# Two 1024-token super-tiles per streamed weight, with recurrence, sample states and attention interleaved between dense matmul pieces

## The chip, the cores and the metric

One Trainium2 chip, all eight NeuronCores, one launch. Core *c* takes prompt sequence *c* (2048 tokens) and sample sequences 16*c* to 16*c*+15 (8 new tokens each). The metric is the device time of the slowest core in microseconds (us). The kernels here sometimes ran in a second, slower state, in which the cores of one die (once of both) had a lower granted clock and took some per cent longer (one execution of the last version: clock 0.79 to 0.80 and 2623 to 2636 us on cores 0 to 3, 0.93 and 2397 to 2402 us on cores 4 to 7); only fast runs are compared here. A ratio is the mean time of one kernel's fast runs over the mean of the other's fast runs of the same rounds, on the same chip, so it is not quite the ratio of the medians that are quoted.

Engines: PE (TensorE, matmuls), PEld (its weight load), DVE (VectorE), ACT (ScalarE), POOL (GpSimd, which here mostly issues DMAs, the weights' casting ones above all) and SP (which issues other DMAs). The program gives each engine one list of instructions, in the order of issue, with waits for the others by semaphores; what that order can cost shows below, where PE's dense work stands 6.47 us behind four transposes that wait.

## The reference, cut to what matters

```python
D_MODEL, SEQ, DEPTH = 1024, 2048, 2
DEC_BATCH, DEC_SEQ = 128, 8                      # sample group: 1024 tokens over the chip
RET_HEADS, RET_DK, RET_DV, RET_CHUNK = 4, 256, 512, 128
SWA_HEADS, SWA_KV_HEADS, SWA_HEAD_DIM, WINDOW, D_FF = 16, 2, 64, 128, 2816

def step(s, qkv):                                # retention, one 128-token chunk
    qc, kc, vc = qkv
    scores = einsum('bihd,bjhd->bhij', qc, kc) * intra[None]
    o = einsum('bhij,bjhe->bihe', scores, vc)
    o = o + einsum('bihd,bhde->bihe', qc, s) * q_decay[None, :, :, None]
    s = s * chunk_decay[None, :, None, None] + einsum('bjhd,bjhe->bhde', kc * k_decay[None, :, :, None], vc)
    return s, o
# ... o is group-normed per head, gated by silu(h @ w_g), and projected by w_o
# layer 1: softmax attention over a window of 128 with one sink per head

for layer in range(DEPTH):
    hp, hs = rms_norm(xp, norm_mix[layer]), rms_norm(xs, norm_mix[layer])
    # layer 0: retention for the prompt (state starts at 0) and for the sample (state_ret given, returned updated)
    # layer 1: sliding-window attention for the prompt, and for the sample with its key/value cache
    xp, xs = xp + yp, xs + ys
    xp = xp + swiglu(rms_norm(xp, norm_ffn[layer]), ffn_w1[layer], ffn_w3[layer], ffn_w2[layer])
    xs = xs + swiglu(rms_norm(xs, norm_ffn[layer]), ffn_w1[layer], ffn_w3[layer], ffn_w2[layer])
```

The sample group's recurrent states are 16 x 4 matrices of 256 x 512 fp32 per core: 33.5 MB to read and as much to write.

## The kernel before

A small scheduler records each operation with the buffers that it reads and writes and derives the semaphore waits. The kernel walks over four 512-token tiles; for each it streams every weight from HBM (fp32, cast to bf16 by the DMA) through a ring of slots. The order in which the program issues is the order of each engine's list.

```python
for t in range(NPT):                     # NPT = 4 tiles of 512 tokens
    ...
    if last:                             # the sample group rides with tile 3
        R_ = layer0(cx, t, False, t % 2, rider=(scx, ...))   # projections share the weights
        layer0(scx, NPT, True, (t + 1) % 2, pre=R_)          # its states, alone
    else:
        layer0(cx, t, False, t % 2)
    for c_ in cxs: rmsnorm(c_, 1)        # a norm is issued in one block
    ffn(cxs, 0)
    rmsnorm(cx, 2)
    layer1(cx, t, False)
    if last: layer1(scx, NPT, True)      # sample attention, alone
    for c_ in cxs: rmsnorm(c_, 3)
    ffn(cxs, 1)

# layer0, the recurrence of head hd beside the projections of head hd + 1
for c in range(nch):
    c_main(hd, c)            # scores, mask, state update, output, group norm and gate
    if q_: q_.pop(0)()       # one projection piece of the next head
    if c > 0: c_tail(hd, c - 1)          # transposes of the chunk before

# the sample's states, one 256x512 state at a time, four buffers in and four out
issue_s0(u); issue_s0(u + 1); issue_s0(u + 2); issue_s0(u + 3)
act(S0bf[u2][:, a, :], S0[ui][:, a, :], AF.Copy, [S0b[ui]], [S0bfb[u2]])
mm(ob[:, :], Qz[:, a, b, :], S0bf[u2][:, a, :], ...)
stt(Sn[ui][:, a, :], S0[ui][:, a, :], cd, pk[:, :], ALU.mult, ALU.add, ...)
dma("pool", srs[b, hd]..., Sn[ui][:, :, :], [Snb[ui]], [], f"sn{ui}")

# attention, one 128-token block and head pair
act(rec[:, ri, :128], db_[:, :128], AF.Identity, ..., bias=esink[:, hp:hp + 1])
recip(rec[:, ri, 128:256], rec[:, ri, :128], ...)            # 128 columns, 128 times
tt(oT[:, hp, qs], nb_[:, :128], rec[:, ri, 128:256], ALU.mult, ...)
```

The softmax here doesn't subtract the row's maximum and nothing guards it: scores larger than these inputs give would overflow.

## Time and profile before

| | before |
|---|---|
| time, median of 3 runs | 2907.16 us (2906.66 to 2914.06) |
| PE busy | 2195 us of 2913 (75%) |
| DVE, ACT busy | 39%, 31% |
| granted clock, mean by core | 0.860 to 0.867 |
| FFN of a tile | 133 and 142 us |
| sample states, alone; sample attention, alone | 270 us; 115 us |

Two more lines of the page count what the weights cost, since the change halves their traffic: packets, bytes into the cores and mean rate, then the traffic of HBM.

```profile
DMA packets 293096, 336.42 MB, mean 115 GB/s; under 512 B 7184, under 2 KB 257808, under 8 KB 292752
...
HBM read 528.55 MB, written 46.79 MB: 198 GB/s over the span
```

A line of the stage tables (here and in the prediction) reads: stretch in us from the span's start, its length, then busy us and instruction count of PE, PEld, DVE, ACT and POOL, the mean granted clock (1.00, called full, is the highest in the records: 512-column matmuls start 0.216 us apart at it and 0.427 at 0.50, called half), the busy share of the DMA engines and GB/s. A timeline line reads: start, length, engine, program line, operation, output and inputs, count, and in brackets the idle time before it with what ended it. A line of waits reads: engine, tile and line that waited, `<-` what ended the wait; us in total, times, longest. In the lines and below: *rope* is the position-dependent rotation of queries and keys on VectorE (its products are `rt`), `sT` the masked scores of a chunk, `S_0`, `S_1` or `S` the buffers of the sample states and `S0f` a state's bf16 copy; the *carried state* is what the second super-tile's recurrence takes over from the first; a *bank* is one of the eight numbered pieces (0 to 7) of `ps`, the kernel's buffer in PSUM, into which PE's matmuls write.

### The profile page before, as it was taken

The page shows a single profiled execution, that of the slowest core. Times are in us where ns is not written, and L with a number is a line of the kernel's source. Part 1 is how long each engine was busy: PE and PEld are TensorE (multiplying, and loading weights), DVE is VectorE, ACT ScalarE, POOL GpSimd, SP SyncE. Part 2 cuts the span into 40 slices and gives each one's busy share as a digit, 9 for nine tenths or more (in the row PEclk, how much of TensorE's full clock was granted, in tenths as well). Part 3 has the DMA queues.
Part 4 walks back from the last instruction along what each step waited for, and adds up shares of the span by engine and source line. Part 5 has one row for each costly group of instructions (what it writes and reads, how often), then busy time and mean ns, then how long its engine had stood idle before and what let it go on. Part 6 is the DMA issues. An engine that isn't in the chain of part 4 may idle for free.

```text
span 2913.1 us, 36426 instructions; the slowest of 8 cores (2885.2 to 2913.1 us)
## 1 busy us (share of the span) xinstructions
PE 2194.7 (75%) x11759; PEld 1031.3 (35%) x11759; DVE 1130.9 (39%) x2050; ACT 895.0 (31%) x1678; POOL 257.3 (9%) x311
## 2 busy tenths in 40 slices
PE   4768876987789868887798689776654499762697
PEld 1323333433334343333243434333211245341353
DVE  4542127136431172265311631645345331271422
ACT  2441134114521251144211520445233221343211
POOL 0000100110001100100011001000111201000010
PEclk9889988998879999999798999898755689895698
DMA  9547881797549827974488369544787878625274
GB/s 197 81 60 101 122 125 30 102 141 149 86 60 138 130 36 108 145 152 73 73 116 129 46 102 139 100 73 77 205 292 264 235 112 127 98 32 111 43 113 97
DMA packets 293096, 336.42 MB, mean 115 GB/s; under 512 B 7184, under 2 KB 257808, under 8 KB 292752
## 3 DMA queue, kind: packets, MB, share of 16 engines
q0 software_dynamic: 256944, 272.89, 59.4%
q1 hardware_dynamic: 35968, 61.20, 6.8%
q8 instruction: 101, 1.65, 0.2%
q14 instruction: 83, 0.68, 0.1%
HBM read 528.55 MB, written 46.79 MB: 198 GB/s over the span
## 4 chain that ended last, share of the span: by engine, by line
PE 60%; DVE 14%; DMA 11%; issue 8%; ACT 6%; DVEq 1%; SPq 0%; ACTq 0%; POOL 0%; POOLq 0%
PE pb L415 59%; DMA wr<-w 5%; DVE arena L424 4%; DVE arena L433 4%; DMA arena<-st_in 4%; ACT arena L421 3%; DVE rstd L433 2%; ACT sq L421 1%; ACT L421 1%; PE pb L418 1%; DVE hT L427 1%; DMA xT<-xTp 1%; DVE arena L427 1%; DVE stat L594 1%; DMA wr<-wo 1%
## 5 line engine op out<-in xcount | busy, mean ns | idle before, releaser
L415 PE MATMUL pb<-hT,wr 128*128 128x512 bf16 x3776 | 911.9, 399 | 81.5 <-DVE hT L427 68.3
L415 PEld LDWEIGHTS pb<-hT,wr 128*128 128x128 bf16 x3776 | 379.4, 101 | 592.2 <-issue 202.9
L415 PE MATMUL pb<-arena,wr 128*128 128x512 bf16 (+1 forms) x2720 | 535.7, 362 | 47.3 <-DMA wr<-w 21.8
L421 ACT ACTIVATE arena<-pb 128x512 bf16<-128x512 f32 (+3 forms) x584 | 319.9, 559 | 718.1 <-PE pb L415 629.4
L415 PEld LDWEIGHTS pb<-arena,wr 128*128 128x128 bf16 x2720 | 255.6, 103 | 323.6 <-issue 84.9
L415 PE MATMUL pb<-arena 128*128 128x128 bf16 (+2 forms) x576 | 146.4, 358 | 277.8 <-DVE arena L424 151.7
L424 DVE TENSOR_TENSOR arena<-arena,pb 128x512 bf16<-128x512 f32 x220 | 133.7, 608 | 526.4 <-PE pb L415 505.3
L436 POOL DMA_DIRECT2D wr<-w x144 | 125.0, 869 | 1350.7 <-PE pb L415 1349.1
L421 ACT ACTIVATE sq<-xT 128x512 bf16<-128x512 f32 x160 | 93.2, 622 | 491.2 <-PE pb L415 335.2
L415 PE MATMUL pb<-wr,hT 128*128 128x512 bf16 x1024 | 234.1, 389 | 0.0
L424 DVE TENSOR_TENSOR xT<-pb,xT 128x512 f32<-128x512 f32 x96 | 66.4, 692 | 419.9 <-PE pb L415 419.9
L421 ACT ACTIVATE arena<-arena 128x512 bf16<-128x512 f32 (+1 forms) x192 | 109.4, 575 | 268.8 <-DMA arena<-st_in 135.0
L415 PEld LDWEIGHTS pb<-arena 128*128 128x128 bf16 x576 | 42.3, 104 | 357.7 <-issue 351.9
L415 PEld LDWEIGHTS pb<-wr,hT 128*128 128x128 bf16 x1024 | 102.4, 100 | 127.9 <-issue 14.7
L424 DVE TENSOR_TENSOR arena<-arena,cbt 128x512 bf16<-128x512 bf16 (+2 forms) x148 | 57.4, 389 | 207.5 <-ACT arena L421 206.6
L415 PE MATMUL pb<-sq,cbt 128*128 128x512 bf16 (+1 forms) x200 | 74.1, 397 | 83.6 <-ACT sq L421 76.9
L427 DVE SCALAR_TENSOR_TENSOR arena<-arena,pb 128x512 f32<-128x512 f32 x128 | 87.3, 687 | 114.4 <-PE pb L415 102.8
L433 DVE RECIPROCAL arena<-arena 128x128 f32<-128x128 f32 (+1 forms) x130 | 127.9, 984 | 2.3 <-ACT arena L421 1.9
L433 DVE RECIPROCAL rstd<-rtmp 128x512 f32<-128x512 f32 (+1 forms) x25 | 71.8, 2873 | 110.8 <-ACT rtmp L421 110.1
L424 DVE TENSOR_TENSOR arena<-arena 128x512 bf16<-128x512 f32 (+2 forms) x136 | 87.7, 666 | 63.1 <-ACT arena L421 63.1
L418 PE MATMUL pb<-cbt,arena 128*128 128x128 bf16 x464 | 45.5, 244 | 79.2 <-DVE arena L1086 46.5
L421 ACT ACTIVATE Sbf<-Sst 128x512 bf16<-128x512 f32 x128 | 75.2, 624 | 97.2 <-PE pb L415 58.6
(79 smaller groups left out, 1623.0 us busy)
## 6 DMA issues: line engine op xcount, KB each, us to landing
wr<-w POOLq DMA_DIRECT2D x112, 1024.0 KB, 12.2
arena<-st_in SPq DMA_DIRECT2D x64, 512.0 KB, 8.0
srs<-arena POOLq DMA_DIRECT2D x64, 512.0 KB, 7.9
wr<-wo POOLq DMA_DIRECT2D x30, 1024.0 KB, 9.6
wr<-wqk POOLq DMA_DIRECT2D x16, 1024.0 KB, 13.3
wr<-wv POOLq DMA_DIRECT2D x16, 1024.0 KB, 11.7
wr<-wg POOLq DMA_DIRECT2D x16, 1024.0 KB, 9.9
wr<-w POOLq DMA_DIRECT2D x16, 768.0 KB, 13.6
```

Source lines behind the costliest of these rows:

```text
L415: S.op("pe", lambda e: e.matmul(out, lhsT, rhs, start=start, stop=stop), r, w)
L418: S.op("pe", lambda e: e.transpose(out, in_, ident), r, w)
L421: S.op("act", lambda e: e.activation(out=out, in_=in_, func=func, bias=bias, scale=scale), r, w)
L424: S.op(eng, lambda e: e.tensor_tensor(out=out, in0=in0, in1=in1, op=op), r, w)
L427: S.op("dve", lambda e: e.scalar_tensor_tensor(out=out, in0=in0, scalar=scalar, in1=in1, op0=op0, op1=op1), r, w)
L433: S.op("dve", lambda e: e.reciprocal(out=out, in_=in_), r, w)
L436: S.op(eng, lambda e: e.dma_start(out=out, in_=in_), r, w, dsem=sem)
L594: S.op("dve", lambda e: e.bn_stats(out=st[:, 0:6], in_=ob), [obb], [sbf])
```

## The change

Its intent: stream each weight twice, not four times; put the sample group's states, its attention and the recurrence beside dense matmuls instead of alone; take the norms apart into steps between other pieces. The core of a diff that replaces nearly the whole program (cuts marked by `...`):

```diff
-        for t in range(NPT):
-            ... one tile of 512 tokens, as above
+        for s in range(2):                           # super-tiles of 2 x 512 tokens
+            ta, tb = T[2 * s], T[2 * s + 1]
+            self.ret_layer(s, cxs, scx if s == 0 else None, ...)
+            if s == 0:   # the sample states: pairs 0 to 15 beside this FFN
+                self.ffn(cxs, 0, [...], sideB)       # sideB -> ret_sample(range(0, 16), ...)
+            else:
+                self.ffn(cxs + [scx], 0, [...], None)
+            self.att_layer(s, cxs, scx if s == 1 else None, [...])
+            ...          # second FFN: sideD -> ret_sample(range(16, 32), ...) where s == 0
+def weave(main, side, lead=0.0):                     # side pieces spread by their stated costs
+    for p in main:
+        out.append(p); cm += p[0]
+        while k < len(side) and cs / ts_ <= cm / tm - 1e-9 + lead:
+            out.append(side[k]); cs += side[k][0]; k += 1
+# retention: the recurrence Rp(h, ti) woven into the projections P(next)
+            for c in range(4):
+                pcs.append((3, lambda n=n: r_o(n)))        # output product, group norm, gate
+                pcs.append((2, lambda n=n: r_su(n)))       # state, accumulated in PSUM banks 4 and 5
+                pcs.append((0.5, lambda n=n: r_sc(n + 1))) # scores of the next chunk, bank 7, mask on DVE
+                pcs.append((1, lambda n=n: r_tl(n - 1)))   # transposes of the chunk before, bank 7
+        # projections: query halves, then key halves, each pair of banks held until its second rope half
+            for which in range(2):
+                for half in range(2):
+                    pcs.append(qk_half(which, half))
+            for c in range(4):
+                pcs.append(vg("v", c))
+        ...
+        # second super-tile: carried state added on DVE
+                    self.tt(sb_[:, :, :], S2, si_[:, :, :], ALU.add, sbk + sib, sbb)
+# sample states: pairs of states, two buffers, updated and stored in place
+        st["S0"] = [self.M.tile(f"S0_{i}", [128, 2, 2, 512], F32, self.xoff[2] + i * 8192) for i in range(2)]
+            if a == 1:
+                for gg in range(2):
+                    self.dma("sp", out_v[...], t[:, gg, :, :], tb, [], f"s0_{i % 2}")
+                load(i + 2)
+# attention: 64-row matmuls, one reciprocal for four head pairs
+            self.tt(r0..., ps[:, 7, :]..., self.esink..., ALU.add, ...)
+            self.recip(r0[:, :], r0[:, :], r0b, r0b)       # 512 columns, 32 times
+# norms: three steps, each issued one piece later
+        self.nq += [s0, s1, s2]
```

## The prediction

Rival 1 went whole: a lower granted clock in the dense stretches, with its sign, with the reason for stretching the range upward (2290 plus 150 is 2440, the range ends at 2490) and with one reason for the chance of 0.97. In the paragraph before "The change part by part" the 3353 ns are those of DVE's reciprocal. Some terms lean on estimates. Tiled matmuls at 69 us instead of 138 suppose that pairs of them overlap, which the kernel before could not show, as it has none. The "about 0.04" for 32 columns is high (they start 0.026 to 0.027 us apart even at half clock). A semaphore hop, from the end on one engine to the start on the other, is a median 0.11 us from PE to DVE and 0.15 from DVE to PE in the trace before. The 35 us of half clock were not worked out from the trace, which shows clock 0.50 from 850 to 860 us, in and after a norm gap.

> **What bounds the kernel now.** I read in this order: cores and dies (is this run undisturbed?), the page's first lines and slices (which engine, when), the chain that ended last, a table of engine busy time by stage, the PE timeline inside single stages, and last the groups with their mean durations. The dies agree within 1 us, so nothing here is a slow state.
>
> The page, then the chain:
> ```profile
> span 2913.1 us, 36426 instructions; the slowest of 8 cores (2885.2 to 2913.1 us)
> ...
> PE 2194.7 (75%) x11759; PEld 1031.3 (35%) x11759; DVE 1130.9 (39%) x2050; ACT 895.0 (31%) x1678; POOL 257.3 (9%) x311
> ...
> PEclk9889988998879999999798999898755689895698
> ...
> PE 60%; DVE 14%; DMA 11%; issue 8%; ACT 6%; DVEq 1%; SPq 0%; ACTq 0%; POOL 0%; POOLq 0%
> ```
> PE is the bound engine, but 718 us of the span (2913 - 2195) it does nothing, and its clock dips wherever it idles; 40% of the chain is other engines and DMA. The stage table of core 2 (columns: stretch, its length, busy us and counts of PE, PEld, DVE, ACT, POOL, granted clock, DMA share, GB/s) shows where:
> ```profile
> 642.00:843.00 201.00, 154.87 (x721) 69.52 (x721) 103.41 (x205) 83.87 (x147) 13.10 (x15) 0.86 0.59 101
> 843.00:976.00 133.00, 123.10 (x536) 53.15 (x534) 29.15 (x39) 19.72 (x32) 15.63 (x18) 0.94 0.87 123
> 976.00:1090.00 114.00, 80.42 (x578) 44.85 (x575) 63.48 (x116) 51.97 (x107) 5.26 (x6) 0.88 0.40 63
> 1090.00:1232.00 142.00, 125.42 (x543) 53.50 (x542) 29.94 (x40) 25.35 (x40) 16.51 (x19) 0.94 0.87 124
> ...
> 2070.00:2340.00 270.00, 125.25 (x420) 42.97 (x420) 125.10 (x177) 91.67 (x153) 50.97 (x70) 0.60 0.86 265
> ...
> 2620.00:2735.00 115.00, 35.66 (x527) 26.91 (x524) 29.70 (x85) 36.23 (x96) 3.63 (x5) 0.57 0.48 93
> ```
> The first four lines are one 512-token tile: retention with its output projection, FFN, attention, FFN. The FFNs are dense; retention loses 46 us and attention 34. The last two lines are the sample group's recurrent states (bound by DMA at 265 GB/s) and its attention: 385 us in which PE works 161 us, at a clock near 0.6.
>
> The PE timeline gives the unit costs and shows what a gap is (start, length, line, operation, count, idle before and its releaser):
> ```profile
> 67.62 3.62 PE L415 MATMUL pb<-hT,wr 128*128 128x512 bf16 x16
> 71.08 0.71 PE L415 MATMUL pb<-arena 128*128 128x128 bf16 x4
> 78.14 0.58 PE L415 MATMUL pb<-arena 128*128 128x512 bf16 x1 [6.36 <-DVE arena L424]
> ...
> 2614.98 3.74 PE L415 MATMUL pb<-hTs_sb,wr 128*128 128x128 bf16 x64
> ```
> In the third line PE stands 6.36 us for the score mask, which DVE runs only after the rope of the next head. A warm 512-column matmul starts every 0.216 us ((3.62 - 0.38 for the last one's own length)/15), a 128-column one every 0.056 ((3.74 - 0.2)/63).
>
> [...]in 5 us windows the clock is 0.50 after each norm gap (850 to 860 us) and 1.00 from 865 on. [...]from 863 to 923 us all four cores of either die are busy 8 us or more of every 10, and all read 1.00. [...]the trace has 58 loads of 1283 ns. [...]the trace has 3353 ns for 128x512, against 692 for an add. [...]
>
> **The change part by part.**
> *PE work* (counts are of the built program of each kernel; they sum to 11759 and 10444). Before: 7780 with 512 columns, 3659 with 128, 320 with 32: 7780 x 0.216 + 3659 x 0.056 + 320 x about 0.04 = 1898 us warm. The measured 2195 us busy thus has about 297 us of half clock in it. After: 7388 full 512-column ones = 1596; 640 tiled 512-column ones (attention by 64 rows or columns, sample states by 32) are 138 us if they don't overlap and 69 in pairs, I take 105; 2224 with 128 = 125; 192 small = 8. Sum 1834. So the floor hardly moves (-64). The gain must come from the 718 us idle and the 297 us cold.
>
> *Weights.* Each is streamed twice, not four times (and wo, q1, wo1 again for the sample). Before, the DMA waits on wr are 5 to 6% of the chain; those 150 us go. The FFN of the first super-tile now also carries half the sample states: 34.6 MB of fp32 weights plus 33.5 MB of states, at the 300 GB/s or so that the queues reached (256944 packets in 59.4% of 16 engines is 108 ns for 2 KB read; 88 ns for 1.7 KB on the hardware queue) is about 220 us, in an FFN that takes PE 256 (1056 matmuls, and 16 pairs of states with 8 each). Tight; states are double-buffered and stored and loaded in place (two transfers of about 8 us each; a pair comes every 16 us and a buffer every second pair, so some 20 us are free). I allow 15 us in each of two FFNs.
>
> *Sample group.* 385 us alone become pieces between dense ones: their PE time is in the floor. Remains about 20 us where the sample attention's small steps outlast the few projections beside them.
>
> *Retention.* A 128-token chunk has 25 units (of 0.216 us) of projection beside 6.5 of recurrence: 6.8 us of PE. The norm-and-gate chain of a chunk in the trace (191.34 to 196.14) took 4.8 us with a table load, so it fits into a period. But the transposes of chunk n-1 stand right behind the scores of n+1 in the same PSUM bank, so each waits for the mask on DVE: 0.29 us plus two semaphore hops, plus what rope (12 x 0.69 per four chunks) has queued there. I put 1.3 us on each of 64 chunks: 83 us. ACT gets 92 table loads for 58 (Sqrt and Silu alternate 43 times for 24, counted in the program): +44 us, on an engine that has room (4.3 us of work plus 1.3 of load per 6.8).
>
> *Attention.* DVE per step: two masks 128x1024 bf16 about 0.7 each (0.417 at 512), add 0.69, reciprocal 3.35, multiply 0.69 = 6.1, with a hop 6.6 us; 8 steps 53 us. Beside it stand 27 us of PE (projections of the other tile) or 22 (wo1, which adds 6 us of DVE). DVE is the bound there: excess (53 - 27) + (59 - 22) = 63 per super-tile, 126 in all. The reciprocals themselves are no cheaper: 128 of 947 ns before (121 us), 32 of 3353 after (107).
>
> *Norms.* They no longer stop everything (10 us each before, 842.9 to 852.9), but their burst on DVE (3.35 + 8 x 0.67 = 8.7 us, behind a Sqrt table) holds up the adds that free two or four PSUM banks: I take 8 us where a two-bank projection follows (three a super-tile), 4 or less elsewhere: 40 per super-tile, 85 with the sample.
>
> *Ends.* Start 45 us (39 before; the constants that the first norm needs now queue behind four weight units), tail 20 (24 before). Between the super-tiles tile 3's input waits for tile 0's store: 15. Half clock after the remaining long gaps: 35.
>
> Sum: 1834 + 65 + 30 + 20 + 83 + 126 + 85 + 15 + 35 = 2293. Predicted **2290 us**.
>
> **The rivals.**
> 1. [...]
> 2. *In-order PE makes side pieces expensive.* Every wait in a side piece now stops dense work too; DVE (about 1090 us busy, as before) and ACT serve both. With 3 us per chunk instead of 1.3 and 10 us per norm: +150, 2440.
> 3. *Everything hides.* Tiled matmuls overlap by pairs, masks are ready, norms cost 2 us: 2130. Speaks for it: the before trace's DVE and ACT are idle 60%.
> 4. *DMA becomes the bound of the first super-tile's FFNs*: +40 us each.
>
> **Range and chances.** The terms for stalls sum to 394 us of which half is judgement: plus or minus 150 around 2290[...]: 2130 to 2490. [...]faster by over 2%: 0.97; within 2%: 0.02; slower: 0.01.
>
> **What would show it.** Right: PE busy near 1900 us with some 10,400 matmuls and 83% of the span; FFN stretches with PE at 95% and clock 1.00 while the states are loaded; attention stretches with DVE over 90% and PE near 50%; 92 table loads; PE waits in retention that name the mask (DVE into sT) in the transposes. Wrong: [...]waits of PE on state loads (rival 4); DVE under 80% in attention; PE waits on the gate chain larger than those on the mask.

## The result, and the profile after

The changed kernel took 2643.32 us (median of 4 runs, 2638.91 to 2651.96) where the kernel before took 2909.25 (4 runs, 2906.66 to 2914.06): ratio 0.9074, 95% interval 0.9039 to 0.9109. It is faster, as predicted, but by 266 us and not by 617; the time lies 353 us above the predicted 2290 and outside the range of 2130 to 2490.

The page of the changed kernel, the lines that answer to those shown of before, and two groups (line, engine, operation, names, shapes, count | busy us, mean ns | idle just before, and what ended it):

```profile
span 2650.9 us, 30100 instructions; the slowest of 8 cores (2614.8 to 2650.9 us)
...
PE 2096.1 (79%) x10444; PEld 927.8 (35%) x10444; DVE 1079.2 (41%) x1698; ACT 751.5 (28%) x1172; POOL 119.5 (5%) x227
...
PEclk9777777989878788898987988899999987889998
...
DMA packets 87220, 211.91 MB, mean 80 GB/s; under 512 B 10752, under 2 KB 13696, under 8 KB 83968
...
PE 57%; DVE 17%; DMA 13%; issue 7%; ACT 5%; DVEq 0%; SPq 0%; ACTq 0%; POOLq 0%
...
L506 ACT ACT_TABLE_LOAD x92 | 118.0, 1283 | 234.5 <-PE ps L499 99.9
...
L503 PE MATMUL ps<-cbt,u 128*128 128x128 bf16 x256 | 29.0, 246 | 138.8 <-DVE sT L509 130.8
```

The packets of all transfers are down from 293096 to 87220, their bytes from 336 to 212 MB, and PE idles 555 us instead of 718. But PE is busy for 2096 us, 262 more than the 1834 of the prediction's floor, with the very count of matmuls it named, so its clock must be lower than foreseen (this core's records read 0.50 for 489 us of the run and 0.81 for 477); DMA is a larger share of the chain than before (13% for 11%); and the transposes of the retention wait 131 us for the mask.

The stage table of core 3: retention, first FFN and attention of the first super-tile, then the same of the second.

```profile
0.00:491.00 491.00, 376.26 (x1664) 168.77 (x1665) 179.61 (x371) 194.50 (x309) 15.14 (x32) 0.82 0.29 57
491.00:839.00 348.00, 301.31 (x1217) 116.03 (x1215) 118.36 (x182) 78.07 (x106) 21.69 (x41) 0.85 0.66 157
839.00:1019.00 180.00, 120.85 (x549) 42.81 (x548) 123.47 (x114) 54.57 (x70) 5.81 (x11) 0.81 0.16 27
...
1377.00:1849.00 472.00, 332.73 (x1598) 151.74 (x1598) 211.36 (x381) 163.64 (x262) 13.03 (x25) 0.86 0.29 64
1849.00:2130.00 281.00, 267.94 (x1614) 137.02 (x1613) 83.13 (x140) 54.47 (x105) 23.14 (x42) 0.98 0.40 65
2130.00:2354.00 224.00, 140.39 (x972) 60.11 (x970) 155.91 (x176) 70.72 (x105) 6.77 (x13) 0.84 0.15 25
```

The second super-tile's FFN is what the prediction wanted everywhere: PE busy 268 of 281 us at clock 0.98, with the sample group's columns in it. The first super-tile's, with the sample states beside it, needs 67 us more. Two stages of retention make 963 us.

One period of the retention in detail (timeline of core 3; DVE between two matmul groups of PE):

```profile
1670.09 0.28 PE L499 MATMUL ps<-q_65,k_67 128*128 128x128 bf16 x2
...
1671.30 1.28 DVE L509 TENSOR_TENSOR rt<-ps,rope_52 128x512 f32<-128x512 f32 x2
...
1673.29 1.22 DVE L509 TENSOR_TENSOR Sbf_79<-ps,Sin_80 128x1024 bf16<-128x1024 f32 x1
1674.42 1.28 DVE L509 TENSOR_TENSOR rt<-ps,rope_52 128x512 f32<-128x512 f32 x2
...
1676.41 0.28 DVE L509 TENSOR_TENSOR sT<-ps,cbt 128x128 bf16<-128x128 f32 x1
...
1676.84 0.58 PE L503 MATMUL ps<-cbt,u 128*128 128x128 bf16 x4 [6.47 <-DVE sT L509]
```

The score product (first line) is done at 1670.4. Its mask (`sT`) needs 0.28 us of DVE, but stands there behind the gate of the last chunk, two rope halves and the addition of the carried state, all issued earlier. The transposes on PE don't need that mask at all: they write to the bank that the mask still has to read. For the kernel's scheduler bank 7 is one buffer, so it orders the transposes' writes behind the mask's read, and the 6.47 us are that order's price. Whether the order could be left out no run here shows: every kernel keeps it. All dense work stands behind the transposes.

The clock, in the stretches of that gap and after it:

```profile
1670.00:1675.00 5.00, 0.37 (x4) 0.10 (x1) 4.21 (x6) 0.58 (x1) 0.00 (x0) 1.00 0.39 77
1675.00:1682.00 7.00, 5.16 (x16) 2.17 (x17) 3.14 (x7) 0.60 (x1) 0.00 (x0) 0.52 0.00 0
```

PE is idle, keeps its full clock for some 5 us, and then has half the clock for 7 us, most of them with matmuls running. So a wait of 6.5 us is followed by 5.2 us of work at half speed, which is another 2.6 us lost.

The waits of core 3 (engine, line, releaser: us in total, times, longest), of PE, and of the queue that issues the state transfers:

```profile
PE ps L503 <- DVE sT L509: 130.8, 55, 6.8
...
PE ps L499 <- ACT S0f_109 L506: 63.7, 15, 12.2
```

```profile
SPq L123 <- DMA srs<-S_0_107: 114.4, 15, 13.6
SPq L123 <- DMA srs<-S_1_108: 95.1, 16, 9.8
```

The first line is the retention's transposes. In the others PE waits for the bf16 copy of a state (`S0f`), the copy for the state's load, and the load, issued into the buffer just stored, for the store to land: 6.8 us a time in the issuing queue, at most 13.6.

Last, the clock of the first run had a third value. On core 3 the records read 0.81 for 477 us of the run, on core 0 for 432, on cores 4 and 5 for 297, on cores 6 and 7 for 148. Core 0 and core 2 in the same stretch of the first retention:

```profile
150.00:250.00 100.00, 79.21 (x389) 38.25 (x395) 41.12 (x93) 48.28 (x75) 1.59 (x3) 0.88 0.19 37
...
150.00:250.00 100.00, 81.34 (x367) 37.55 (x367) 41.61 (x92) 44.59 (x69) 1.59 (x3) 0.75 0.20 38
```

Core 2 (the second line), at a mean clock of 0.75 for 0.88, needs more PE time for fewer matmuls: 81.3 us for 367 against 79.2 for 389. That is a lower granted clock, as in the prediction's rival 1, for a part of the run and some of the cores.

### The profile page after: what moved, and what is told of

It is laid out like the page before. It is cut to its first block, busy times and chain, and to the rows that moved or that the text cites. A ratio compares the mean times of both kernels' runs of the same rounds, so it can differ in the third digit from the quotient of the medians.

```text
span 2650.9 us, 30100 instructions; the slowest of 8 cores (2614.8 to 2650.9 us)
## 1 busy us (share of the span) xinstructions
PE 2096.1 (79%) x10444; PEld 927.8 (35%) x10444; DVE 1079.2 (41%) x1698; ACT 751.5 (28%) x1172; POOL 119.5 (5%) x227
## 2 busy tenths in 40 slices
DMA packets 87220, 211.91 MB, mean 80 GB/s; under 512 B 10752, under 2 KB 13696, under 8 KB 83968
## 4 chain that ended last, share of the span: by engine, by line
PE 57%; DVE 17%; DMA 13%; issue 7%; ACT 5%; DVEq 0%; SPq 0%; ACTq 0%; POOLq 0%
PE ps L499 56%; DMA S_0_107<-st_in 4%; DMA srs<-S_0_107 3%; DVE rt L509 2%; DMA S_1_108<-st_in 2%; DVE rstd L518 2%; PE ps L503 1%; DVE rec_124 L518 1%; DMA spt<-spar 1%; DVE h_44 L512 1%; DVE rec_125 L518 1%; ACT on L506 1%; DMA srs<-S_1_108 1%; DVE h_45 L512 1%; DVE stat L681 1%
## 5 line engine op out<-in xcount | busy, mean ns | idle before, releaser
L499 PE MATMUL ps<-h_44,wr 128*128 128x512 bf16 x1824 | 453.4, 408 | 35.2 <-DVE rt L509 10.4
L499 PE MATMUL ps<-h_45,wr 128*128 128x512 bf16 x1824 | 453.6, 407 | 26.0 <-DMA wr<-w 9.5
L499 PEld LDWEIGHTS ps<-h_44,wr 128*128 128x128 bf16 x1824 | 184.5, 103 | 282.9 <-issue 120.6
L499 PEld LDWEIGHTS ps<-h_45,wr 128*128 128x128 bf16 x1824 | 183.3, 103 | 273.7 <-issue 121.9
L499 PE MATMUL ps<-aT_105,wr 128*128 128x512 bf16 x704 | 170.9, 401 | 6.9 <-DVE x_62 L509 6.9
L509 DVE TENSOR_TENSOR aT_103<-s_104,ps 128x512 bf16<-128x512 f32 x88 | 60.4, 687 | 278.2 <-PE ps L499 242.9
L509 DVE TENSOR_TENSOR aT_105<-s_106,ps 128x512 bf16<-128x512 f32 x88 | 60.5, 687 | 262.6 <-PE ps L499 228.4
L499 PE MATMUL ps<-aT_103,wr 128*128 128x512 bf16 x704 | 164.5, 392 | 2.6 <-DVE aT_105 L509 1.7
L499 PE MATMUL ps<-wr,h_44 128*128 128x512 bf16 (+1 forms) x576 | 142.8, 400 | 9.8 <-DVE rt L509 8.7
L227 POOL DMA_DIRECT2D wr<-w x152 | 80.4, 531 | 1398.7 <-PE ps L499 1287.5
L499 PE MATMUL ps<-wr,h_45 128*128 128x512 bf16 (+1 forms) x584 | 142.8, 395 | 0.0
L506 ACT ACTIVATE s_104<-ps 128x512 f32<-128x512 f32 x88 | 52.5, 596 | 314.1 <-PE ps L499 305.3
L506 ACT ACTIVATE s_106<-ps 128x512 f32<-128x512 f32 x88 | 52.5, 596 | 243.3 <-PE ps L499 233.1
L509 DVE TENSOR_TENSOR x_61<-ps,x_61 128x512 f32<-128x512 f32 x80 | 55.3, 691 | 158.0 <-PE ps L499 158.0
L681 DVE BATCH_NORM_STATS2 stat<-ps 128x6 f32<-128x512 f32 x68 | 47.4, 697 | 155.1 <-PE ps L499 132.7
L499 PEld LDWEIGHTS ps<-aT_105,wr 128*128 128x128 bf16 x704 | 71.1, 102 | 100.5 <-issue 34.7
L499 PE MATMUL ps<-sq,cbt 128*128 128x512 bf16 (+1 forms) x200 | 56.0, 388 | 62.3 <-ACT sq L506 60.7
L499 PEld LDWEIGHTS ps<-aT_103,wr 128*128 128x128 bf16 x704 | 68.7, 100 | 90.7 <-issue 24.9
L499 PEld LDWEIGHTS ps<-wr,h_44 128*128 128x128 bf16 x576 | 56.8, 106 | 75.5 <-issue 49.1
```

What stands on the lines that cost most here:

```text
L227: self.S.op("pool", (lambda o_, i_: (lambda e: e.dma_start(out=o_, in_=i_)))(dst, src), (), [b], dsem=f"w{self.next % self.NSEM}")
L499: self.S.op("pe", lambda e: e.matmul(out, lhsT, rhs, start=start, stop=stop, skip_group_check=skip), r, w)
L506: self.S.op("act", lambda e: e.activation(out=out, in_=in_, func=func, bias=bias, scale=scale), r, w)
L509: self.S.op("dve", lambda e: e.tensor_tensor(out=out, in0=in0, in1=in1, op=op), r, w)
L681: S.op("dve", lambda e: e.bn_stats(out=st[:, 0:6], in_=ob), [obb], [sb])
```

## The experiments

Theories for the missing 353 us: (A) the sample states' two buffers; (B) the retention's in-order PE behind VectorE's queue; (C) the stretches at 0.81; (D) attention, norms and start, mis-sized; (E) the half clock that follows gaps, as a cost of its own. The rivals of A: the transfers are too slow anyway. Of B: the recurrence's pieces lie in the wrong places, or VectorE simply has too much to do. All 15 runs are told, four to a chip and three on the last. "Control" is the unaltered changed kernel, run with the second four: 2638 us (median of 3 fast runs; 3 were slow), ratio to before 0.9042 (0.9015 to 0.9070). Only these four have the control on their own chip; the ratios to before of the other runs are compared with 0.9042 across chips. Since 0.81 comes to some cores of some runs, single cores that show none of it in either profiled run are compared as well (core 7 of the control: 2614 us; the mean of its six such cores: 2607 us).

**Spread of the recurrence's pieces.**

```diff
-                pcs.append((3, lambda n=n: r_o(n)))
+                pcs.append((1.5, lambda n=n: r_o(n)))
-                    pcs.append((0.5, lambda n=n: r_sc(n + 1)))
+                    pcs.append((2, lambda n=n: r_sc(n + 1)))
```

> Only the placing of the recurrence's pieces between the projections changes: one projection of eight matmuls now stands between the scores of chunk n+1 and the transposes of chunk n-1, which use the same PSUM bank. Theory A (the transposes wait for the mask that frees the bank): the 131 us that PE waited for DVE on sT falls below 40 us, the two retention stages shorten by 60 to 130 us together and the kernel by as much, to about 2520 to 2580 us. Rival (DVE's queue is the limit in retention, and the wait only moves to the output matmul that reads the masked scores): the waits reappear there and the time falls by under 25 us.

Correct, 2588.53 to 2595.20 us in three fast runs (one was slow), ratio 0.8895 (0.8874 to 0.8915): 0.015 below the control, 43 us, of which the absence of 0.81 in its profiled run is a part: core 7, which has none in either run, takes 2591 us for 2614, 23 us less. The waits of the transposes fell from 59 to 40 us in the first retention of core 7, and the gain of the stage is 24 us (441 for 465). In the second they fell from 92 to 74 and the stage from 478 to 469. The wait of the output matmul, where the rival looked for it, did not grow (14 us for 18), yet the gain is of the rival's size. Places matter, but do not end the wait.

**A dependence for each half of a state pair.**

```diff
-        st["S0"] = [self.M.tile(f"S0_{i}", [...], F32, ...) for i in range(2)]
+        st["S0"] = [self.M.tile(f"S0_{i}", [...], F32, ..., 2) for i in range(2)]
-                    self.dma("sp", t[:, gg, :, :], st_v[...], [], tb, f"s0_{i % 2}")
+                    self.dma("sp", t[:, gg, :, :], st_v[...], [], [tb[gg]], f"s0_{i % 2}_{gg}")
```

> Each half of a pair of sample states gets its own dependency handle and semaphore, so that the two loads of a pair no longer wait for each other on the issuing queue; bytes, buffers and matmuls are the same. Theory A (the round trip of store, load, load on one queue sets the pace of the first super-tile's FFNs): the 72 us of PE gaps before the state matmuls fall below 30 us, the two FFN stages (348 and 358 us) come near 300 us each, and the time falls by 60 to 110 us to about 2530 to 2580 us. Rival 1 (the DMA engines are full): the loads take longer than 4.4 us in turn and the time falls by under 20 us. Rival 2 (two buffers are too few, whatever the order): about half of the gain, 30 to 50 us.

Correct, 2582.92 us (2579.68 to 2585.02), ratio 0.8862 (0.8845 to 0.8880). The waits for the state copy went from 85 us in the control to 50, the two FFNs of the first super-tile from 342 and 349 us to 323 and 331 (core 7, which takes 2573 us for 2614). That is part of A, and of the size that its rival 2 named: two buffers are too few.

**Zero norm gains (wrong result).**

```diff
-            self.stt(o[:, kc, :NT], cx.x[:, kc, :NT], self.gain(gi, kc), ...
+            self.stt(o[:, kc, :NT], cx.x[:, kc, :NT], 0.0, ...
```

> The norm's gain is replaced by zero, so nearly every matmul streams zeros; wrong result on purpose, instructions, transfers and waits the same. Theory A[...]: no 0.81 in the record,[...] since in retention part of it is hidden behind other waits I expect 30 to 80 us, 2560 to 2610 us. Rival[...]: 0.81 remains and the time is the same within 10 us.

2617.08 us (2613.28 to 2622.94), ratio 0.8976 (0.8956 to 0.8997), and no core at 0.81. But no other profiled run of that call showed 0.81 either, with ordinary data. So whether 0.81 goes away with zeros was not tested, and the run is inconclusive; it serves as a figure for a run without 0.81, with no waits moved.

**A quarter of the attention's reciprocal (wrong on purpose).**

```diff
-            self.recip(r0[:, :], r0[:, :], r0b, r0b)
+            self.recip(r0[:, :128], r0[:, :128], r0b, r0b)
```

> The 32 reciprocals of the prompt's attention work on 128 of 512 columns (wrong result on purpose): 0.95 us instead of 3.35 each, 77 us less on DVE. Theory A (DVE is the bound of the attention stages, as predicted): the two attention stages shorten by 60 to 80 us and the time by as much, to about 2565 to 2585 us. Rival (PE's in-order waits on norms and on scores bound these stages): under 30 us.

2555.07 to 2570.05 us in three fast runs (one was slow), ratio 0.8798 (0.8755 to 0.8842): the attention stages came down from 179 to 153 us in the first super-tile and from 224 to 189 in the second (core 7). The first of them here (the control's line stands with the filler run below):

```profile
808.00:961.00 153.00, 109.40 (x550) 40.99 (x549) 85.66 (x114) 54.49 (x70) 5.81 (x11) 0.87 0.19 32
```

Of the 77 us taken from VectorE 61 show. In the attention VectorE sets the pace for most of the time, as predicted, and the reciprocals are a large part of its work.

**Control.** No edit.

> The changed kernel, unaltered, as a control on the chip of these runs. Two readings of the 0.81 granted clock that its first run showed for 148 to 477 us on each core, and that none of the first four experiments showed. If it belongs to that chip or that moment, this run shows none of it, PE busy time comes down from 2096 by up to 80 us (477 us at 0.81 instead of 1.00, nine tenths busy), and the time is 2590 to 2625 us. If it belongs to the kernel (any edit that thins it takes it away), it is here again and the time is 2635 to 2655 us. Either way the half clock should stay at 460 to 530 us a core.

2638 us in its fast runs, and 0.81 is back, on two of eight cores. The core view of its profiled run, core 0 and core 3 (span and mean granted clock):

```profile
core 0: 2592.8 us, clock 0.905
...
core 3: 2643.1 us, clock 0.884
```

Cores 2 and 3 have 298 us at 0.81 and take 2634 us on average; the six without any take 2607. So 0.81 belongs neither to the kernel alone nor to one chip: it comes in some runs, to some pairs of cores, and 298 us of it cost about 27, as far as so few cores can tell (the six differ among themselves by 26 us). Of my two readings neither is quite right: the time is that of the second, since one pair in that state is enough where the slowest core counts, but six of eight cores look like the first. C explains some 30 of the 353 us. Half clock was 457 to 512 us on each core, as expected.

**Transposes in a shared bank.**

```diff
-            bv = ps[:, 7, :].bitcast(BF16)
+            bk, bb = self.pb(DN)              # one of the four projection banks
+            bv = bk.bitcast(BF16)
```

> One part of the retention alone: the transposes of the gated chunk go to a bank of the shared pool instead of bank 7, which the score product and its mask use, so they no longer wait for the next chunk's mask in the VectorE queue. Theory (bank 7 turns a long VectorE queue into a wait of the in-order TensorE): the waits of the transposes, 131 us in the changed kernel and 48 plus 90 us by stage, fall below 30 us; with them go some 30 windows of half clock at about 1.7 us each; the time falls by 80 to 130 us against the control. Rival (the VectorE queue itself is too long, the wait only changes its place to the output product that needs the same mask): the output product's waits, 16 us now, grow to over 80 us and the time falls by less than 40 us.

Correct, ratio 0.8884 (0.8819 to 0.8949), 2580.2 and 2600.9 us in two fast runs: 46 us below the control, between theory and rival. The waits of the transposes, whatever ended them, fell from 151 us to 11 (core 7, 59 and 92 to 7 and 4), but the projections' grew from 46 to 132, for the most part waits for rope results. The rival named the wrong place: the output product's waits only went from 18 to 29 us. The control's lines (core 7; the first has no successor here, the second's is shown with the next run):

```profile
PE ps L503 <- DVE sT L509: 142.2, 55, 6.8
...
PE ps L499 <- DVE rt L509: 19.1, 2, 10.4
```

**Carried state through PE.** On top of the last edit, the carried state is put into the accumulation banks by 16 identity products of a high and a low bf16 half; ACT copies out.

```diff
+            if s == 1 and ci == 0:
+                for a in range(2):
+                    for j, (t_, tb_) in enumerate((Sbf[n % 2], lo[h % 2])):
+                        self.mm(ps[:, 4 + a, :], cb[:, CB_ID:CB_ID + 128], t_[:, a, :], j == 0, False, ...)
-                    self.tt(sb_[:, :, :], S2, si_[:, :, :], ALU.add, sbk + sib, sbb)
+                self.act(sb_[:, :, :], S2, AF.Copy, sbk, sbb)
```

> The transposes in a pool bank, as in the run before last, and besides, in the retention of the second super-tile, the carried state is put into the accumulation banks by TensorE (identity products of a high and a low bf16 half, 16 matmuls in all) and copied out by ScalarE, so that VectorE no longer adds it at 1.22 us for each of 56 chunks: 68 us of VectorE work less. The results stay right. Theory (with the bank shared out, what the projections wait for in the retention is the VectorE queue): their waits for the rope, 82 us in that stage with the bank shared out, fall below 50 us, the stage comes down from 435 us to 390 to 410 us, and the time is 20 to 40 us below that of the shared-out bank alone (2562 us on its undisturbed die). Rival (the wait is the rope's own chain and bank hold, not the length of the queue): the waits stay above 70 us and the time moves by less than 8 us.

Correct, 2590.42 us (2588.81 to 2592.65), ratio 0.8876 (0.8861 to 0.8891): no change to 0.8884, whose interval is wide (19 us to either side); the cores without 0.81 take 2566 us on average for 2561 with the shared bank alone. The PE waits on the rope, of the run before (core 7) and of this one (core 1):

```profile
PE ps L499 <- DVE rt L509: 83.5, 20, 10.4
```

```profile
PE ps L499 <- DVE rt L509: 73.3, 21, 10.4
```

These lines are of both retentions; in the second, the only one that the edit touches, the waits are 54 and 46 us. (The expectation took all of them for that stage, and counted 56 additions of the carried state where the trace has 28.) VectorE's work in the second retention went from 211 to 181 us, not by 68, and its length from 435 to 437. So the rival holds as far as this goes: 30 us less in VectorE's queue bought nothing there.

**The start in order.** Small constants first; only the first weight unit is fetched before tile 0 has landed.

```diff
+        self.dma("pool", self.cb[:, :], DR["cb"][:, :], (), [self.cbb], "c1")
+        self.dma("sp", self.sp[:, :], DR["spar"][:, :], (), [self.spb], "c0")
         load_x(0)
+        self.ring.gate = T[0].xb      # the other units wait for tile 0
```

> The start alone: the small constants are loaded first and only the first weight unit is fetched before the first tile has landed; the other units wait for it. In the changed kernel the first norm waits 39.5 us for a small parameter load behind 12 MB of other transfers, and the first projection starts at 52.4 us. Theory (transfers of the start share the engines): the first norm starts at 15 to 22 us, the first projection at 28 to 35 us and the time falls by 12 to 22 us. Rival (the weights are what the start waits for anyway): the first projections then wait for their units, and the time falls by less than 6 us.

Correct, 2619.16 us (2611.42 to 2631.04), ratio 0.8986 (0.8947 to 0.9024), 16 us below the control, though the intervals touch. The first norm started at 16.8 us instead of 40.9 and the first projection at 30.7 instead of 52.4 (core 3; the older figures are of the first run). All eight cores of its profiled run had 141 to 295 us at 0.81, where only two of the control had any, so the edit may be worth more. Some was given back: the second tile, now behind the weights, landed near 50 us, and PE waited 7.9 us for its squares.

**Four buffers for the state pairs.**

```diff
+        st["S0"] = [... for i in range(4)]    # each half with its own dependence
-                load(i + 2)
+                load(i + 3)                   # into the buffer whose store was issued a pair ago
```

> The sample states get four buffers in place of two, each half with its own dependence, and a load is issued three pairs ahead, into the buffer whose store was issued one pair before. Theory (the store has to land before the next load of the same buffer, 12.8 to 13.6 us a time in the queue, and the cast waits for that load): the waits of the query product on the cast state, 64 us in the changed kernel, fall below 15 us, the two feed-forward stages of the first super-tile come down from 348 and 358 us to 290 to 310 us each, and the time falls by 60 to 100 us, twice what the separate halves alone gave (a fall of 24 to 60 us, according to the control). Rival (the transfers are too slow by themselves): the DMA is then the bound and the stages stay above 325 us; the time falls by no more than the separate halves gave.

Correct; 2531.09, 2532.73 and 2546.92 us in the fast runs, ratio 0.8700 (0.8659 to 0.8741): 100 us below the control. The two FFNs of the first super-tile (core 7):

```profile
463.00:750.00 287.00, 263.69 (x1216) 108.27 (x1215) 115.33 (x183) 78.10 (x106) 21.68 (x41) 0.97 0.83 192
929.00:1229.00 300.00, 268.62 (x1221) 109.54 (x1219) 116.69 (x185) 84.31 (x117) 18.02 (x34) 0.97 0.71 169
```

287 and 300 us against 342 and 349, PE dense at clock 0.97, DMA engines 83% busy at 192 GB/s in the first. PE's wait for the state copy, in the control and here (core 7):

```profile
PE ps L499 <- ACT S0f L506: 85.4, 36, 8.4
```

```profile
PE ps L499 <- ACT S0f L506: 7.2, 9, 3.1
```

The transfers were not too slow; A holds.

**A quarter of the norms' reciprocal (wrong on purpose).**

```diff
-        ... AF.Sqrt, ..., bias=EPS, scale=1.0 / D)
-        self.recip(self.rstd[:, :NT], self.rtmp[:, :NT], ...)
+        ... AF.Sqrt, ..., bias=1.0, scale=0.0)
+        self.recip(self.rtmp[:, :128], self.rtmp[:, :128], ...)
```

> Wrong result on purpose: every norm takes its reciprocal over a quarter of the columns (about 0.9 us in place of 3.35), with a constant in place of the sum of squares so that all values stay finite; all its other work is done. It sizes the norms: 20 prompt norms by 2.4 us are 49 us of VectorE. Theory (a norm lies on the path wherever its tile is wanted next, as at the attention's entry, the start and the end): half or more of that shows, and the time falls by 20 to 45 us against the control. Rival (the eight multiplications and the squares are what is waited for, or other work covers it): less than 12 us.

2592.43 to 2611.58 us in three fast runs (one was slow), ratio 0.8925 (0.8883 to 0.8967): 34 us below the control. Of 49 us of VectorE taken away, two thirds show, and perhaps more, since all cores of the profiled run had 144 to 295 us at 0.81. The norms are on the path, about as predicted.

**Filler matmuls in the attention.** Eight matmuls on constants before each of 32 attention steps.

```diff
+            bk, bb = self.pb(DN)
+            for i in range(8):
+                self.mm(bk, cb[:, CB_ID:CB_ID + 128], cb[:, CB_QM:CB_QM + 512], True, True, [cbb], [bb])
```

> Before each of the 32 prompt attention steps that wait for VectorE, eight matmuls of 512 columns on constants are added, written to a projection bank and read by nobody: 1.7 us of TensorE each, 55 us in all, put where TensorE waits 2 to 4 us anyway. It tells whether the half clock costs anything where another engine sets the pace. Theory A (the half clock after a short gap is a cost of its own[...]): the half clock in the two attention stages falls from 68 and 71 us to under 30 and the time falls by 10 to 30 us in spite of the added work. Theory B (VectorE sets the pace in the attention): the half clock falls too, but the time moves by less than 8 us either way. Theory C (the added work is simply paid): the time grows by 20 to 55 us.

Correct, 2648.67 to 2655.87 us in the fast runs, ratio 0.9084 (0.9064 to 0.9104), 12 us above the control, though the intervals touch; cores 6 and 7, without 0.81 in both runs, take 4 and 6 us more. The attention of the first super-tile (core 7) in the control and here:

```profile
807.00:986.00 179.00, 120.45 (x549) 42.90 (x548) 123.48 (x114) 54.62 (x70) 5.81 (x11) 0.81 0.17 27
```

```profile
806.00:990.00 184.00, 138.39 (x678) 52.48 (x677) 123.71 (x114) 54.35 (x70) 5.81 (x11) 0.90 0.16 26
```

The clock rose from 0.81 to 0.90 and half clock fell from 68 to 38 us, PE was busy 18 us longer (30 us more work at full clock), and the stage got 5 us longer (the second one 7). Theory A of that run is refuted, and little of the added work is paid, against C. Where VectorE sets the pace, less half clock bought nothing here; a small gain could hide behind the added work.

**The repairs together:** spread, bank, carried state, four buffers, and the start with tile 1 loaded ahead of the later weights.

> The repairs together, all with right results: recurrence pieces spread, transposes in a pool bank, carried state through TensorE, four state buffers with halves, and the start in order with the second tile's load ahead of the later weights. If the causes are separate their gains add (about 45 for the bank and the spread, 25 for the carried state, 100 for the buffers, 25 for the start): 2420 to 2460 us. Rival (they relieve the same wait, or the time freed turns into new waits of the VectorE queue): 2480 us or more.

Correct; 2447.04 and 2450.18 us in the fast runs (two were slow), ratio 0.8390 (0.8369 to 0.8410): 190 us below the control. Some of that is the absence of 0.81, which no core of its profiled run shows: its cores take 2443 us on average, 164 less than the control's six. The edits alone gave about 46 us (bank), nothing (carried state), 100 (buffers), 16 (start) and 23 (spread, core 7), 185 in sum: most of it adds, and the time is in the expected range, though the 25 us put down to the carried state were never there. Both retentions still take 435 us and more.

**Another order of projections,** on top of that.

```diff
             for which in range(2):
                 for half in range(2):
                     pcs.append(qk_half(which, half))
+                for c in (0, 1) if which == 0 else (2, 3):
+                    pcs.append(vg("v", c))
-            for c in range(4):
-                pcs.append(vg("v", c))
```

> The repaired version with one more edit: two value projections stand between the query halves and the key halves, so that the two pairs of banks held for the rope do not follow one another; VectorE's work is the same. Theory (the hold of the four projection banks is what the projections wait for): the waits of the projections on the rope, 71 us, fall below 35 us, the two retention stages come down from 435 and 438 us to 400 to 420 us each, and the time is 2395 to 2425 us. Rival (VectorE's queue is too long whatever the order): the waits stay above 55 us or come up elsewhere in those stages, and the time stays at 2435 us or more.

Correct, 2421.30 us (2420.37 to 2421.54), ratio 0.8287 (0.8275 to 0.8299), 30 us below the repairs together; the retentions take 424 and 417 us for 435 and 437. PE's waits on the rope in the repaired kernel and with the new order (core 7):

```profile
PE ps L501 <- DVE rt L511: 71.3, 21, 10.4
```

```profile
PE ps L501 <- DVE rt L511: 45.6, 16, 7.6
```

They did not fall below 35 as I had expected, and the time lies within the expected range. So the hold of the four projection banks was part of the wait: with the same VectorE work, an order in which the two held pairs do not follow each other takes a third of it away. (Some came back elsewhere: PE's waits for the value copies of ScalarE went from 3 to 15 us.)

**A quarter of the rope (wrong on purpose),** in the old order.

```diff
-                            self.tt(rt[:, 0, :], b1, rp[:, m0, :], ...)
+                            self.tt(rt[:, 0, :128], b1[:, :128], rp[:, m0, :128], ...)
```

> Wrong result on purpose: the repaired version with the rope's multiplications on a quarter of the columns, in the old order. VectorE loses about 0.4 us of each of 256 multiplications, some 100 us in the two retention stages. If VectorE's time is what the projections wait for, these stages come down by 25 to 45 us each and the time is 2365 to 2400 us. If only the order of holds counts, shorter multiplications shorten the holds as well and help too, but a run of the order alone must then give as much with VectorE's work unchanged. If neither (the waits belong to ScalarE or to the in-order chain of scores, output and norm), the time stays at 2430 us or more.

2402.27 to 2403.84 us in three fast runs, ratio 0.8225 (0.8209 to 0.8242), just above the expected range: the first retention 411 us, the second 417, 24 and 20 us less than in the repaired kernel, with 25 us less VectorE work in each (the expectation took 50). In the second super-tile the order alone gives as much as the shorter rope; in the first, 13 us more come from the shorter rope. A shorter rope also shortens the holds, so this does not part the two entirely; together with the run before it, hold and latency of the rope are the likelier cause of the wait, and not VectorE's total.

**And the states' last transposes later:** the new order, with the transposes that end a head of the sample states issued after the next head's first pieces.

```diff
             if i % 8 == 0:
                 out.append((1, lambda h=h: head(h)))
-                out.append((1, lambda h=h: head2(h)))
             out.append((1, lambda i=i: cast(i)))
+            if i % 8 == 0:
+                if i != pairs[0]:
+                    out.append((1, lambda h=h: fin2(h - 1)))
+                out.append((1, lambda h=h: head2(h)))
```

> The repaired version with the new order and one more repair: the transposes that end a head of the sample states are issued after the next head's first pieces instead of right after the group norm they wait for (21 us of waits in the two feed-forward stages). All results right. If these waits are on the path it is 10 to 20 us below the new order alone: 2380 to 2410 us. If TensorE finds another wait there, it equals the new order alone within 5 us.

Correct, 2402.50 to 2404.49 us in three fast runs (one was slow), ratio 0.8226 (0.8213 to 0.8240): 18 us below the new order alone. The two FFNs of the first super-tile take 279 and 293 us for 289 and 297 (core 7), but the waits that the edit aimed at fell only from 21 to 13 us, so not all of the 18 is explained by them. It is the fastest right version found here, 237 us below the changed kernel by the ratios (0.9042 - 0.8226 = 0.0816, of 2910 us), of which some 30 are again the absence of 0.81 (its cores take 2398 us on average, 209 less than the control's six), and 17.7% below the kernel before.

## Why the prediction was right or wrong

I worked out for each stage how much PE work it holds: every stretch in which PE was busy times the clock granted in it, summed over the instruction and clock records of core 7 (the 11 us of busy time before the first clock record are counted at half clock: matmuls start 0.43 us and more apart there, 0.216 later). Stage length = this work + PE idle + what the lower clock cost (busy less work). The control, core 7, and the last version beside it:

| stage | work at full clock | length, control | idle | lower clock | predicted beyond work | length, last version |
|---|---|---|---|---|---|---|
| retention 1 | 302 | 465 | 132 | 31 | 143 in both: start 45, masks 83, change-over 15 | 425 |
| FFN 1a, with states | 260 | 342 | 66 | 16 | 15 | 279 |
| attention 1 | 96 | 179 | 59 | 24 | 63 | 183 |
| FFN 1b, with states | 264 | 349 | 67 | 18 | 15 | 293 |
| retention 2 | 291 | 478 | 138 | 48 | (above) | 421 |
| FFN 2a | 264 | 282 | 13 | 5 | 0 | 281 |
| attention 2 | 117 | 224 | 84 | 23 | 83 | 224 |
| FFN 2b | 264 | 297 | 28 | 5 | 20, the tail | 293 |
| sum | 1858 | 2614 | 586 | 170 | 339, and 85 norms and 35 half clock anywhere | 2398 |

(The columns sum to within 2 us by rounding.) The run took 2643 us, 29 more than this core, and the share of 0.81 (some 30 us) can account for that.

*The PE floor: right.* 1834 was predicted, 1858 measured, with the 10,444 matmuls named. The weights' traffic halved and is out of the chain; the second super-tile's FFNs are as dense as foreseen.

*The sample states: the first step that failed.* The prediction said: a transfer takes about 8 us, a pair comes every 16, "a buffer every second pair, so some 20 us are free. I allow 15 us in each of two FFNs." The excess of these two FFNs is 167 us and not 30 (norms come on top of both). I counted the time of the transfers and not their order: the load is issued behind the store of the same buffer in one in-order queue, each pair has one dependence for both halves, and the copy needs the whole pair. Four buffers with halves, loads issued three pairs ahead, and the same transfers, took 100 us away. My rival 4, "DMA becomes the bound", has the right wait and nearly the size (+40 each) but the wrong reason: the DMA engines could do it.

*The retention: the second.* The mechanism was named, transposes behind the mask in one bank, and its size was off: "1.3 us on each of 64 chunks: 83 us" were 142 us in 55 waits, 2.6 each, because rope and the carried state's addition lie before the mask (6.5 us of wait in the period shown). And it was not all. Sharing the bank out gave 46 us and moved the wait to the projections, whose banks rope holds; this second wait, 46 us before and 132 after, the prediction does not have. Rival 2 ("3 us per chunk", 2440) has the right mechanism, and 2.6 us per wait is near its size. Beyond its work the retention lost 350 us in both stages; start, masks and change-over were to be 143. All repairs bring it to 245 (of the last version's 846, 601 are its own work).

*The half clock: the third.* "Half clock after the remaining long gaps: 35" was 170 us (core 7), 47 of them in the attention, where the filler run found nothing to gain. So about 88 us of the miss, net of those, are lower clock in other stages, mostly in the retention (79). I read it as no separate cause, since it follows the gaps that the first two steps missed; no edit outside the attention tests that. I had counted only long gaps. In the first run of the changed kernel, of 102 isolated gaps of 2 to 3 us 57 were followed by half clock within 3.41 us of their end, and of 313 gaps of 0.3 to 1.5 us only 1 (all cores; see the last section).

*Attention, norms, start: right, more or less.* Attention lost 190 us beyond its work with its norms, for 146 without; DVE was busy 123 of 179 us over the stage, 69%, and 95% and more only in part of it (916 to 956 us in the control, core 7). By the prediction's own sign, under 80% would have meant wrong; the sign was badly chosen, since it is the run with the short reciprocal that shows who sets the pace. Besides, the norms' reciprocals showed 34 us; the start was 52 us to the first projection for the predicted 45.

*The clock of 0.81, rival 1: partly.* I gave a lower clock in the dense stretches one in five, and it came in a small way, 0.81 on some pairs of cores for 148 to 477 us; it cost some 30 us, not hundreds. What brings it no run here shows.

*Sum.* Beyond work: retention 207 over its terms, states' FFNs 137, attention 44, last FFNs 31; less the 120 that the prediction had put anywhere (norms and half clock) is 299; with 24 for the floor and 29 for 0.81 and slowest core (2643 less 2614) that makes 352 of the 353. The sum closes by construction, since the table splits one core's time; what the runs tested of it are the states' buffers, the mask wait and its move, the norms' reciprocals and the start. What in the retention remains (245 us beyond its work in the last version) is not settled beyond the two waits named.

## What to carry to other kernels

When side work is woven into a dense in-order stream, list for each side piece everything that its first instruction waits for, including the bank or buffer that another engine still has to leave, and read how much that engine has queued before; moving a dependence from one bank to another helps only in part if another wait on the same engine stands behind it (here 46 us, where 140 of waits had gone). For in-place buffers count the round trip of store, landing and load in the issuing queue, not the transfer time, and give enough buffers to cover it (here two did not, four with halves did). And price a PE gap with the half clock that follows it (here after 57 of 102 isolated gaps of 2 to 3 us and 83 of 93 of 3 to 4), but only where PE sets the pace: in the attention less half clock gained nothing.

## What the clock records show

- Half clock came in multiples of 3.41 us: in the first run of the changed kernel of 78 stretches on core 3, 37 lasted 3.41 us, 24 twice that and 13 three times. One stretch that is full of matmuls costs 1.7 us of work. On its eight cores, isolated PE gaps (no other gap over 0.3 us ended in the 6.8 us before, clock 1.00 when the gap began) were followed by half clock within 3.41 us of their end so often: up to 1.5 us, 1 of 313; 1.5 to 2 us, 10 of 28; 2 to 3 us, 57 of 102; 3 to 4 us, 83 of 93; over 4 us, 196 of 196. So here a gap of 2 to 3 us was enough more often than not. (In the kernel before it was not: 28 of 74.)
- 0.81 came to pairs of cores (2 and 3 alone in the control, 6 and 7 alone in the run with the carried state through PE), for about 147, 295 or 430 to 477 us, in some runs of a kernel and not in others. It ended while the load went on: on core 3 of the first run it was over from 460 to 673 us, with PE busy for 176 of the 209 us from 463 to 672. The densest kernel here (clock 0.93, 2404 us) showed none in its profiled run, nor did the profiled runs of the first four experiments, all on one chip.
- 298 us of 0.81 on two cores cost 27 us against the six others in the control, and 294 us on two cores cost 20 in the run with the carried state through PE.
